# Hybrid trunk with sixteen experts: the last expert's round in an order of its own, one transfer for the state space's table, the values' weights split by channel blocks

## The chip, the core and the metric

The kernel runs on one core of a Trainium2 chip. The metric is the device time of one execution in microseconds; lower is better. The engines meant below are PE (matrix products), DVE (vector), ACT (scalar functions and copies), POOL (GpSimd, here small operations and indirect transfers) and SP (which only issues transfers). Each works through its own instructions in order and waits on semaphores for the others.

## What is computed

One layer of a decoder trunk on 1040 tokens (16 learned ones ahead of 1024) of width 1024, in float32:

```python
h = concat([meta, x])
z = rms_norm(h, norm_mix_g)
proj = z @ w_in            # conv a, conv gate, q, k, v, forget logits, state-space input
y_conv = conformer_conv(cv_a, cv_g, ...)
y_att  = forgetting_attention(q, k, v, f_lg + fgate_b)     # 8 heads of 64, causal
y_ssm  = s5_mixer(s_u, ...)                                # 16 groups of 16 channels, 64 states
h = h + concat([y_conv, rms_norm(y_att), rms_norm(y_ssm)]) @ w_out
h = h + hier_moe(rms_norm(h))    # 4 groups of 4 experts; top group, top 2 in it
return rms_norm(h, final_norm_g)[:, 16:]
# an expert: (silu(t @ w1[e]) * (t @ w3[e])) @ w2[e], weighted by its gate; FF = 256
```

## The kernel before

Every float32 product is made of three products of rounded numbers: each operand is split into a high part and the rest, and `mm3` (lines 281 to 283, one for each of the three) adds high by rest, rest by high and high by high into one bank. So every weight that comes in is first copied by ACT with rounding (the high part) and then subtracted by DVE (the rest).

**Front part.** A scheduler orders the instructions of projection, convolution, state space and attention by the priorities of the code. `load_w` loads a block of the input projection's weights and splits it: ACT line 356, DVE line 357. For the values it is called twice for each of two halves of 260 columns, each time with four blocks of 128 channels, so that one split works on 128x1040; the 24 products of each block of tokens (`KT_`, nine of them) use the channel blocks k = 0 to 7 in turn, as lines 281, 282 and 283 for each k. Between these products the scheduler puts the steps of the state space: products L1923, DVE lines 1930 to 1946, POOL lines 1932 to 1947, then products L1955 and L1958. DVE also works at the convolution there (L480).

`TT` is a table of the state space's kernel. Its 240x256 numbers are written to a scratch tensor `k_d` (L1894, L1895) and read back as eight windows that overlap, shifted by 16 rows each: eight transfers of 128 KB (L1900), each into one slice of `tj`. ACT L1901 copies the whole to `TT`, and PE's L1955 uses it.

**Experts.** The sixteen experts are worked through in an order written out by hand (`tc.manual_schedule()`), one round each. For expert e, a block b of up to 128 tokens and a half hf of the columns, the names of the steps are: f0, f1 the first products of block 0 and 1 (24 of 512 columns each); g0, g1 the gate (ACT L1289, DVE L1291 and L1292); u0, u1 the turn of the gated numbers (PE L1298); v0, v1 their split (ACT L1303, DVE L1304); w0, w1 the split of the two halves of w2 (ACT L1350, DVE L1351); s00, s01 the second products of block 0 of the expert before (6 of 512 columns each), s1 those of its block 1; e00 to e11 the evictions of the expert before (DVE L1513 in the last rounds). Block 1 is under a condition; of the last four experts (numbers 12 to 15) only expert 15 has a second block in this data.

The rows of tokens that belong to none of the last four experts go out as dense rows. The rows of experts 12 to 15 are held in tiles `hr[e]`, to which the evictions add; then each is normed (`norm_steps`: ACT L1404 squares, POOL L273 and L275 the root, DVE L1409 the product) and written with an indirect transfer of POOL (`result`, L1447). Norm steps of the rows that are ready are kept in a list `later`, and `tick(n)` takes n of them at the places that `TICKS` names. What no round takes is done behind the last round (`tick(99)`), then come expert 15's second products, its evictions, and the norms and results of experts 14 and 15.

## Time and profile before

| what | us |
|---|---|
| runs shown: median (lowest to highest of 3) | 863.53 (860.25 to 863.63) |
| the profiled execution's own time | 861.33 |
| its span in the profile | 859.7 |
| PE busy | 785.4 (91% of the span) |
| DVE busy | 592.2 (69%) |
| ACT busy | 433.5 (50%) |
| POOL busy | 243.1 (28%) |

The span is the stretch from the first to the last instruction that the profile has; the execution's own time is 1.6 us longer. Times within the trace are counted from the span's start. PE's mean granted clock is 0.964 of its full 2.4 GHz.

### The profile page before, as it was taken

Reading aid. Unit: us, or ns where it says so; the run is one execution under the profiler, and the core shown is the slowest. Engines: PE = TensorE matmul, PEld = TensorE weight load, DVE = VectorE, ACT = ScalarE, POOL = GpSimd, SP = SyncE. Lnnn points to the kernel's source line nnn. Section 1 sums busy time; section 2 is a strip of 40 time slices with the busy share of each in tenths; the row PEclk is TensorE's granted clock in tenths of the full one; section 3 lists DMA queues with packets and bytes.
Section 4 is the critical chain, followed back from the end, with each engine's and each line's share of the span. In section 5 each row is a group of like instructions: output and inputs, shape, how many; then the busy total and the mean of one; then the engine's idle time right before and its main releaser. Section 6 shows DMA issues by size and latency. Waiting matters only on the chain. (4 is left out here: it accounts for less than half of the span.)

```text
span 859.7 us, 13252 instructions
## 1 busy us (share of the span) xinstructions
PE 785.4 (91%) x4496; PEld 638.1 (74%) x4497; DVE 592.2 (69%) x1298; ACT 433.5 (50%) x788; POOL 243.1 (28%) x359
## 2 busy tenths in 40 slices
PE   6799988999999999999999999968999999897873
PEld 4698978989899955566657888846887886675652
DVE  4972898887745376666625336587779777897995
ACT  5512354434334166556564322145569565786861
POOL 2189978730001000000002110013224223223144
PEclk9999998999999999999999999978999999999985
DMA  9126131122320042012233334417699979979862
GB/s 279 33 63 125 51 99 39 30 64 73 101 74 1 13 148 99 30 70 75 74 99 80 122 123 147 148 51 256 213 296 286 279 237 267 302 242 269 323 265 108
DMA packets 88861, 121.49 MB, mean 141 GB/s; under 512 B 14828, under 2 KB 69899, under 8 KB 88786
## 3 DMA queue, kind: packets, MB, share of 16 engines
q1 hardware_dynamic: 81730, 101.46, 37.3%
q0 software_dynamic: 7056, 19.09, 8.3%
q8 instruction: 40, 0.66, 0.3%
q14 instruction: 35, 0.29, 0.1%
HBM read 100.64 MB, written 26.52 MB: 148 GB/s over the span
## 5 line engine op out<-in xcount | busy, mean ns | idle before, releaser
L281 PE MATMUL psum<-arena,arena 128*128 128x512 f32 (+6 forms) x872 | 309.4, 355 | 7.9 <-DVE arena L1513 2.4
L282 PE MATMUL psum<-arena,arena 128*128 128x512 f32 (+6 forms) x872 | 303.0, 348 | 3.4 <-DVE arena L357 3.3
L283 PE MATMUL psum<-arena,arena 128*128 128x512 f32 (+6 forms) x872 | 302.1, 348 | 0.0
L281 PEld LDWEIGHTS psum<-arena,arena 128*128 128x128 f32 (+1 forms) x872 | 166.7, 191 | 27.4 <-issue 3.9
L282 PEld LDWEIGHTS psum<-arena,arena 128*128 128x128 f32 (+1 forms) x872 | 166.9, 191 | 18.7 <-DVE arena L357 3.9
L283 PEld LDWEIGHTS psum<-arena,arena 128*128 128x128 f32 (+1 forms) x872 | 166.1, 191 | 17.2 <-DVE arena L1279 0.4
L1351 DVE TENSOR_TENSOR arena<-arena,arena 128x1024 fp32r<-128x1024 f32 x96 | 113.5, 1220 | 12.7 <-ACT arena L1350 11.9
L1350 ACT ACTIVATE arena<-arena 128x1024 fp32r<-128x1024 f32 x96 | 98.7, 1072 | 0.0
L722 DVE CUSTOM_DVE_ANT_0 arena<-psum,arena 128x144 bf16<-128x144 f32 (+6 forms) x112 | 55.2, 507 | 47.4 <-PE psum L720 24.2
L777 ACT ACTIVATE arena<-psum,arena 128x512 f32<-128x512 f32 (+4 forms) x112 | 59.2, 539 | 47.8 <-PE psum L774 30.9
L780 PE MATMUL psum<-arena 128*65 128x512 f32 (+4 forms) x224 | 82.8, 455 | 0.5 <-ACT arena L777 0.5
L273 POOL TENSOR_SCALAR arena<-arena 128x1 f32<-128x1 f32 (+2 forms) x37 | 7.9, 213 | 253.9 <-ACT arena L897 71.9
L1315 POOL DMA_INDIRECT h_d<-arena x17 | 34.1, 2007 | 126.5 <-DVE arena L1279 55.1
L1278 ACT ACTIVATE arena<-psum 128x512 fp32r<-128x512 f32 x64 | 38.4, 604 | 27.3 <-PE psum L1272 27.3
L480 DVE SCALAR_TENSOR_TENSOR psum<-arena,psum 128x1024 f32<-128x1024 f32 x40 | 51.4, 1286 | 0.7
L1279 DVE TENSOR_TENSOR arena<-psum,arena 128x512 fp32r<-128x512 f32 x64 | 43.6, 684 | 11.6 <-ACT arena L1278 11.6
L717 PE MATMUL psum<-arena 128*128 128x144 f32 (+6 forms) x112 | 51.4, 483 | 0.0
L490 POOL TENSOR_TENSOR arena<-arena 128x512 f32<-128x512 f32 x36 | 48.5, 1370 | 6.6 <-ACT arena L487 6.6
L769 PE MATMUL psum<-arena 128*128 128x512 f32 (+4 forms) x112 | 47.8, 427 | 2.7 <-ACT arena L777 2.4
L1272 PE MATMUL psum<-arena 128*128 128x128 f32 x256 | 37.8, 281 | 11.6 <-DVE arena L1279 5.2
L1272 PEld LDWEIGHTS psum<-arena 128*128 128x128 f32 x256 | 30.4, 144 | 22.6 <-DVE arena L1304 7.3
L487 ACT ACTIVATE arena<-arena 128x512 f32<-128x512 f32 x40 | 28.4, 722 | 34.6 <-POOL arena L490 24.1
(302 smaller groups left out, 1249.0 us busy)
## 6 DMA issues: line engine op xcount, KB each, us to landing
arena<-in_exp_w_dram SPq DMA_DIRECT2D x64, 512.0 KB
arena<-in_exp_w_dram SPq DMA_DIRECT2D x16, 1024.0 KB
arena<-in_x_dram SPq DMA_DIRECT2D x16, 512.0 KB
arena<-in_w_in_dram SPq DMA_DIRECT2D x14, 512.0 KB
arena<-cr_d SPq DMA_DIRECT2D x8, 520.0 KB
arena<-in_w_out_dram SPq DMA_DIRECT2D x8, 512.0 KB
h_d<-arena SPq DMA_DIRECT2D x8, 512.0 KB
t_d<-arena SPq DMA_DIRECT2D x8, 512.0 KB
```

What stands on the lines that cost most here:

```text
L281: PE.matmul(out=acc, lhsT=lh[k], rhs=rh[k], start=(k == 0), stop=False)
L282: PE.matmul(out=acc, lhsT=lh[k], rhs=rl[k], start=False, stop=False)
L283: PE.matmul(out=acc, lhsT=ll[k], rhs=rh[k], start=False, stop=(k == n - 1))
L480: V.scalar_tensor_tensor(out=yc, in0=ub[:, m, w:w + NX], scalar=cwt[:, m, w:w + 1], in1=yc, op0=OP.mult, op1=OP.add)
L490: G.tensor_tensor(out=yp[:, a:a + 512], in0=yp[:, a:a + 512], in1=o, op=OP.add)
L717: PE.matmul(out=sp, lhsT=QS[:, i * 128 - 128:i * 128], rhs=KS[:, a:b], start=True, stop=not last)
L722: V.tensor_tensor_reduce(out=jk_b()[:, :b - a], in0=sp, in1=nrow[:, a:b], scale=1.0, scalar=-3.0e38, op0=OP.add, op1=OP.max, accum_out=mp[ ...
L777: S.activation(out=pt, in_=sp, func=AF.Exp, bias=ccol[:nk, j, h:h + 1])
L780: PE.matmul(out=po[:, q0 - 512 * g:512], lhsT=vt[:nk, j, h, :], rhs=pt, start=j == 0, stop=j == last, skip_group_check=True)
L1272: PE.transpose(tp[:, k, :], xg[:, c:c + 128], ident)
L1350: S.activation(out=h[:, cs], in_=raw[:, cs], func=AF.Copy)
L1351: eng.tensor_tensor(out=l[:, cs], in0=raw[:, cs], in1=h[:, cs].bitcast(F32), op=OP.subtract)
```

## The change

Four things change.

- **The table.** The eight transfers to `tj` become one of 128x8x256, with a negative stride over the windows.
- **The values' weights.** `load_w` can split in parts. For the values it does so in four, one for each block of 128 channels (128x260), and the calls have a higher priority for the scheduler (`at_priority(-150)`).
- **The last round.** For expert 15, `ORDER` is replaced by `LAST`, in which the numbers are ticks. f1 stands behind s00, s01 and u0, and g1 stands behind w1 and s1. `late67`, which puts the norms of rows 4 to 7 and of experts 12 and 13 on the list, is called at the round's start.
- **The end.** The second products of expert 15's block 0 stand ahead of u1, the squares of 12, 13 and 14 ahead of v1, and what is left of the norms and all results of experts 12 and 13 behind the last eviction.

```diff
-    def load_w(col, n, k0=0, k1=KD, later=False):
+    def load_w(col, n, k0=0, k1=KD, later=False, parts=1):
...
         def split():
-            S.activation(out=h, in_=raw, func=AF.Copy)
-            V.tensor_tensor(out=l, in0=raw, in1=h.bitcast(F32), op=OP.subtract)
+            for i in range(parts):
+                ks = slice(kk // parts * i, kk // parts * (i + 1))
+                S.activation(out=h[:, ks], in_=raw[:, ks], func=AF.Copy)
+                V.tensor_tensor(out=l[:, ks], in0=raw[:, ks], in1=h[:, ks].bitcast(F32), op=OP.subtract)
...
     for half in (1, 0):
-        wv = [load_w(1536 + 260 * half, 260, 4 * q, 4 * q + 4) for q in range(2)]
+
+        with at_priority(-150):
+            wv = [load_w(1536 + 260 * half, 260, 4 * q, 4 * q + 4, parts=4) for q in range(2)]
...
 TICKS = (
     dict(f1=1, s00=1, g0=1, x01=1, w0=1, v0=1, e01=1, x10=2, w1=1, b0=1, b1=1, x11=1),
-    dict(f1=1, x00=1, s00=1, g0=1, t10=2, x01=1, g1=1, s01=1, v0=1, e00=1, e01=1, s1=1, x10=1,
-         t11=2, w1=1, u1=1, b0=1, b1=1, end=4),
 )
+
+LAST = "f0 2 s00 1 w0 g0 1 s01 e00 2 u0 v0 e01 1 f1 w1 2 s1 1 g1 2 e10 e11 2".split()
...
-        3: {"ga": late67},
...
-            for w in ORDER + ["end"]:
+            for w in ORDER + ["end"] if e + 1 < NE else []:
...
-        tick(99)
         e = NE - 1
+        late67()
+        for w in LAST:
+            if w.isdigit():
+                tick(int(w))
+            else:
+                steps[w][0](e)
...
+        do_second(e, 0, 0)
         do(n14[:4])
-        do_second(e, 0, 0)
         do_second(e, 0, 1)
+        do_turn_gate(e, 1)
+        tick(2)
+        do_gate_turned(e, 1)
+        do_evict(e, 0, 0)
         do_second(e, 1, None)
-        do_evict(e, 0, 0)
         do_evict(e, 0, 1)
+        tick(2)
         do(n15[0][:3])
-        do(n14[4:])
         do_evict(e, 1, 0)
         do_evict(e, 1, 1)
+        tick(99)
+        do(n15[1][:3])
+        do(n14[4:])
         for b in range(2):
             result(e - 1, b)
-        do(n15[1][:3])
         for b in range(2):
             do(n15[b][3:])
             result(e, b)
...
-        for j in range(8):
-
-            SY.dma_start(out=tj[:, j, :], in_=dram(k_d, (7 - j) * 16 * 256, [[256, 128], [1, 256]]))
+
+        SY.dma_start(out=tj, in_=dram(k_d, 7 * 16 * 256, [[256, 128], [-16 * 256, 8], [1, 256]]))
```

How the instructions stand now is shown at three places. Line numbers of the changed kernel are 2 to 12 higher: the split's DVE line 357 is 359 there, L480 is 482, L1931 to L1946 are L1943 to L1958, L1289 is L1293, L1303 is L1307, L1350 is L1354, L1404 is L1408 and L1447 is L1451.

On DVE in the front part, around the second split of the values' first half, the order before was as follows (the split is the row with 128x1040):

```order
L1943 TENSOR_TENSOR arena_61<-arena_61 128x390
L480 SCALAR_TENSOR_TENSOR psum<-arena_61,psum 128x1024
L1946 TENSOR_TENSOR arena_61<-arena_61 128x390
L480 SCALAR_TENSOR_TENSOR psum<-arena_61,psum 128x1024 x2
L1931 TENSOR_TENSOR arena_61<-psum,arena_61 128x390
L357 TENSOR_TENSOR arena_84<-arena_61,arena_83 128x1040
L480 SCALAR_TENSOR_TENSOR psum<-arena_61,psum 128x1024
```

In the changed kernel the same stretch reads:

```order
L1958 TENSOR_TENSOR arena_61<-arena_61 128x390
L359 TENSOR_TENSOR arena_84<-arena_61,arena_83 128x260
L482 SCALAR_TENSOR_TENSOR psum<-arena_61,psum 128x1024
L359 TENSOR_TENSOR arena_84<-arena_61,arena_83 128x260 x3
L1943 TENSOR_TENSOR arena_61<-psum,arena_61 128x390
L482 SCALAR_TENSOR_TENSOR psum<-arena_61,psum 128x1024 x2
```

The split has four parts, and they stand ahead of two operations (one of the convolution, L480, and L1931) that were ahead of it.

On ACT in the last round, from the gate of block 0 (the first 128x256 row, L1289) to the split of block 1's turned gate (the second L1303), the order before was as follows; rows with 128x1024 of L1350 are w0 and w1, those of L1404 are squares:

```order
L1289 ACTIVATE arena_61<-psum 128x256
L1404 ACTIVATE arena_61<-arena_61 128x1024
L1289 ACTIVATE arena_61<-psum 128x256
L1350 ACTIVATE arena_60<-arena_61 128x1024
L1303 ACTIVATE arena_2690<-psum 128x256
L1404 ACTIVATE arena_61<-arena_2879 128x1024 x2
L1404 ACTIVATE arena_61<-arena_61 128x1024 x2
L1350 ACTIVATE arena_60<-arena_61 128x1024
...
L1303 ACTIVATE arena_2690<-psum 128x256
```

In the changed kernel, from the same gate on:

```order
L1293 ACTIVATE arena_61<-psum 128x256
L1408 ACTIVATE arena_61<-arena_61 128x1024
L1307 ACTIVATE arena_2707<-psum 128x256
L1354 ACTIVATE arena_60<-arena_61 128x1024
...
L1293 ACTIVATE arena_61<-psum 128x256
L1408 ACTIVATE arena_61<-arena_2896 128x1024
...
L1408 ACTIVATE arena_61<-arena_2896 128x1024
L1408 ACTIVATE arena_61<-arena_61 128x1024 x3
...
L1408 ACTIVATE arena_61<-arena_61 128x1024
L1307 ACTIVATE arena_2707<-psum 128x256
```

Between the gate of block 1 and the split of its turned numbers stand six squares (two each of experts 12, 13 and 14); before, four squares and w1 stood there, and none of expert 14.

On POOL at the end, results of experts 12 and 13 (the first L1447 reads `arena_2879`, a tile of expert 12) stood ahead of the root for expert 14 (128x2) and for the two blocks of expert 15 (128x1):

```order
L275 TENSOR_TENSOR arena_61<-arena_61 128x4
...
L1447 DMA out_dram<-arena_2879,arena_61 1024x1024
...
L1447 DMA out_dram<-arena_61 1024x1024
...
L273 TENSOR_SCALAR arena_61<-arena_61 128x2
L275 TENSOR_TENSOR arena_61<-arena_61 128x2
...
L273 TENSOR_SCALAR arena_61<-arena_61 128x1
```

In the changed kernel the roots come first, that of expert 14 ahead of that of 12 and 13 (128x4):

```order
L275 TENSOR_TENSOR arena_61<-arena_61 128x2
L273 TENSOR_SCALAR arena_61<-arena_61 128x4
L275 TENSOR_TENSOR arena_61<-arena_61 128x4
...
L275 TENSOR_TENSOR arena_61<-arena_61 128x1
...
L1451 DMA out_dram<-arena_2896,arena_61 1024x1024
...
L1451 DMA out_dram<-arena_61 1024x1024
```

All results, those of 12 and 13 too, now stand behind the root of expert 15's first block; the root of its second block follows the results of 13.

## Rows read from the trace of the kernel before

**Rows 1.** Busy time by stretch: length, PE, PEld, DVE, ACT, POOL, PE's clock, DMA, GB/s.
```profile
300.00:400.00 100.00, 96.41 (x530) 59.03 (x529) 67.01 (x197) 62.04 (x106) 0.00 (x0) 1.00 0.23 80
```

**Rows 2.** Timeline of SP: start, duration, instruction; the table's transfers.
```profile
118.46 3.94 SPq L1900 DMA_DIRECT2D arena<-k_d  x8
```

**Rows 3.** Timeline of ACT: the table's copy, with the idle time before it.
```profile
125.40 1.91 ACT L1901 ACTIVATE arena<-arena 128x2048 f32<-128x2048 f32 x1 [2.83 <-DMA arena<-k_d]
```

**Rows 4.** Timeline of PE: the first product with the table.
```profile
127.36 0.49 PE L1955 MATMUL psum<-arena,arena 128*128 128x128 f32 x2 [3.58 <-ACT arena L1901]
```

**Rows 5.** Busy time by stretch, behind the waits of rows 4 and 9.
```profile
129.00:131.00 2.00, 2.00 (x8) 2.00 (x8) 1.10 (x1) 2.00 (x4) 0.17 (x1) 0.50 0.03 2
149.00:152.00 3.00, 3.00 (x15) 2.77 (x14) 2.96 (x4) 1.73 (x5) 2.12 (x3) 0.50 0.63 176
```

**Rows 6.** Timeline of SP: one transfer of 512 KB (128x1024) from a scratch tensor.
```profile
196.10 0.34 SPq L1984 DMA_DIRECT2D arena<-y_d  x1
```

**Rows 7.** Timeline of ACT: the operation that waits for that transfer.
```profile
199.93 1.07 ACT L1985 ACTIVATE arena<-arena 128x1024 f32<-128x1024 f32 x1 [1.96 <-DMA arena<-y_d]
```

**Rows 8.** Timeline of DVE ahead of the second split of the values.
```profile
143.63 2.60 DVE L480 SCALAR_TENSOR_TENSOR psum<-arena,psum 128x1024 f32<-128x1024 f32 x2
...
146.61 1.30 DVE L357 TENSOR_TENSOR arena<-arena,arena 128x1040 fp32r<-128x1040 f32 x1
```

**Rows 9.** Timeline of PE: the values' products before and behind the wait.
```profile
145.43 0.28 PE L281 MATMUL psum<-arena,arena 128*128 128x260 f32 x1
147.97 0.39 PE L282 MATMUL psum<-arena,arena 128*128 128x260 f32 x1 [2.25 <-DVE arena L357]
```

**Rows 10.** Timeline of DVE: the state space's next steps.
```profile
159.61 0.56 DVE L1930 TENSOR_TENSOR arena<-psum,arena 128x390 f32<-128x390 f32 x1 [3.54 <-PE psum L1923]
...
184.61 0.43 DVE L1930 TENSOR_TENSOR arena<-psum,arena 128x260 f32<-128x260 f32 x1 [0.79 <-PE psum L1923]
```

**Rows 11.** Timeline of POOL: the last step ahead of PE's L1958.
```profile
173.43 1.03 POOL L1944 TENSOR_TENSOR arena<-arena 128x390 f32<-128x390 f32 x1
```

**Rows 12.** Timeline of PE: that product.
```profile
175.63 0.71 PE L1958 MATMUL psum<-arena 64*128 64x128 f32 x4
```

**Rows 13.** Timeline of PE in the last round: first and last of f1, u1, and two second products.
```profile
820.87 0.39 PE L281 MATMUL psum<-arena,arena 128*128 128x512 f32 x1
...
826.17 0.39 PE L283 MATMUL psum<-arena,arena 128*128 128x512 f32 x1
...
831.81 0.69 PE L1298 MATMUL psum<-arena 128*128 128x128 f32 x2 [2.24 <-DVE arena L1304]
...
842.43 0.63 PE L281 MATMUL psum<-arena,arena 128*128 128x512 f32 x1
842.86 0.63 PE L282 MATMUL psum<-arena,arena 128*128 128x512 f32 x1
```

**Rows 14.** Timeline of ACT in the last round: two squares.
```profile
817.59 1.06 ACT L1404 ACTIVATE arena<-arena 128x1024 bf16<-128x1024 f32 x1
...
818.77 1.06 ACT L1404 ACTIVATE arena<-arena 128x1024 bf16<-128x1024 f32 x1
```

**Rows 15.** Timeline of DVE in the last round.
```profile
824.68 0.42 DVE L1292 TENSOR_TENSOR arena<-arena,psum 128x256 f32<-128x256 f32 x1
...
829.00 1.22 DVE L1351 TENSOR_TENSOR arena<-arena,arena 128x1024 fp32r<-128x1024 f32 x1
...
835.31 2.48 DVE L1409 SCALAR_TENSOR_TENSOR arena<-arena,arena 128x1024 f32<-128x1024 f32 x2
...
846.25 1.41 DVE L1513 SCALAR_TENSOR_TENSOR arena<-psum,arena 128x512 f32<-128x512 f32 x2
```

**Rows 16.** Timeline of POOL at the end: results of the last experts.
```profile
837.05 1.67 POOL L1447 DMA_INDIRECT out_dram<-arena,arena  x1 [2.51 <-DVE arena L1409]
...
847.66 2.13 POOL L1447 DMA_INDIRECT out_dram<-arena  x1 [0.91 <-DVE arena L1513]
...
853.25 0.96 POOL L1447 DMA_INDIRECT out_dram<-arena  x1 [0.30 <-POOLq L1618]
```

## What the change will do, forecast before it ran

> **What bounds the kernel now.** I read the page first, for where each engine is busy, then the busy times by stretch, then the timelines around the three places that the diff touches. From the values' products to the experts PE is nearly without gaps: in a typical stretch of the middle it is busy 96.41 of 100 us at full clock, and no other engine is above 68 [rows 1]. There a microsecond that PE no longer waits in the front part should come out at the end. In the last 45 us it is another matter: PE waits for DVE and ACT, and the end is set by the chain from the last eviction over the last results of POOL. The reader is to see three things: two holes in PE's work in the front part, each with a stretch of low clock behind it; the order in which ACT takes the squares in the last round; and what POOL still has to send when the last eviction is done.
>
> **The table.** The eight transfers are issued from 118.46 on, over 3.94 us [rows 2]. ACT starts its copy at 125.40, after 2.83 us of waiting for them, and takes 1.91 [rows 3]; PE then starts at 127.36, after 3.58 us of idleness [rows 4]. So from the first issue to the last landing it is 6.94 us. One issue takes 0.34 us [rows 6], so 3.6 us of issuing fall away, but the bytes stay. No row shows one transfer of 1 MB. From below: one of 512 KB took 199.93 − 196.10 = 3.83 us from its issue to the operation that waited for it [rows 6, 7]; 1 MB in that time would be here by 122.3, which gains 3.1 us at most. From above: 6.94 again, no gain. In between, half the bytes more at half that transfer's whole rate (another 1.9 us) gives 5.7, so ACT starts at about 124.2. I take 1.2 us of gain. PE still idles over 2 us then, so I leave the low clock behind it as it is (8 products in 2 us at 0.50 [rows 5]).
>
> The Trainium skill, "DMA: Bandwidth & Descriptors", section "Anatomy of one DMA — SWDGE (gpsimd) path", fits a transfer's time with a fixed 2.0 us and the bytes at 436 GB/s; for 1 MB that is 4.4 us, an estimate, and what that section measured is another queue than SP's. By that fit the gain would be 2.5 us and the total 1.3 us lower than mine. The 512 KB transfer would by that fit take 3.2 us; the trace has 3.83 [rows 6, 7], so the fit is too short here.
>
> **The values' weights.** PE waits 2.25 us at 147.97 for DVE's split of the second four channel blocks [rows 9]. That split of 128x1040 starts at 146.61 because the convolution's operations and one step of the state space stand ahead of it [rows 8]. In the new order the first part stands before the convolution's operation that started at 143.63 and the other three behind it. One operation of 260 columns takes 0.43 us at most [rows 10], so the parts are done at about 144.1 and from 145.6 to 146.4; PE, which was at 145.43 [rows 9] at the first product that needs another block, takes three products for each. So the 2.25 us go. The clock fell to 0.50 behind this wait: 15 products in 3 us [rows 5], work that at full clock is done in 1.5 us, so 1.5 us go too. The second half has smaller waits of the same kind; I take 0.4. In all 4.1 us.
>
> Against it: twelve more operations for DVE and twelve for ACT. Four of 0.43 are 1.7 us where 1.30 stood [rows 8, 10], 0.4 more for each of four splits and 1.6 over both halves. In the first half the 3.54 us in which DVE waits for PE at 159.61 hide that [rows 10]; if PE comes earlier, this cover shrinks to nothing, and DVE's convolution and state-space steps are what is late next. The second point is POOL: its last step ahead of PE's L1958 ends at 173.43 + 1.03 = 174.46, and PE came to L1958 at 175.63, only 1.2 us later [rows 11, 12]. PE that is 4 us early waits for it up to 2.8 us, unless POOL's chain, which begins behind PE's and DVE's work at 159.61, moves forward as well. I give back 0.8 us for both, with bounds of 0 and 3. **Front part: −1.2 − 4.1 + 0.8 = −4.5 us**, between −1.1 and −7.2.
>
> **The last round.** f1 began at 820.87, with f0 done, and ran without a gap: its 24 products from 820.87 to 826.17 are 0.23 apart [rows 13]. Now s00 and s01 come first (12 products, 2.8 us, to 823.6), then u0, which needs g0 from DVE. g0 was done there at 824.68 + 0.42 = 825.1, and w0's 1.22, which stood behind it at 829.00, is now ahead of it [rows 15]: u0 starts at about 826.3. PE idles 2.7 us, and f1 with the 24 products ends at 832.1. Behind an idleness of 2.24 us PE's clock was low until after 842.86, where products stood 0.43 apart [rows 13]; a spell of ten such products adds 2.0, and f1 ends at 834.1. Before, it was done at 826.6.
>
> g1 follows, then on ACT the six squares at 818.77 − 817.59 = 1.18 each [rows 14], 7.1 us in all, ahead of v1. So v1 starts at 839.7, or 841.7 with the spell. PE has only the 12 products of block 0 and u1 meanwhile, idles several microseconds, and takes the last 12 products of block 1 at 0.43 rather than 0.23 (5.2 us instead of 2.8). With DVE's two last evictions, 1.41 [rows 15], the last one is done at 848.4. At full clock the products of 12's rows on DVE set it, since 12's root is now behind 14's on POOL: squares done at 839.7, two roots of about 1 us each, two products 2.48 [rows 15], two evictions, 845.8. Before it was 846.25 + 1.41 = 847.7. **So −1.9 to +0.7; I hold the low clock to be three times as likely, +0.1.**
>
> **The end.** Before, from 847.7 to the end of the last result at 853.25 + 0.96 = 854.2 it was 6.5 us, in which POOL sent three results; those of 12 and 13 had gone ahead, the first at 837.05 [rows 16]. Now there are five results, with a root between. DVE has six products left behind the last eviction, 1.2 each [rows 15], so the last result is sent no earlier than 7.2 us behind it and takes 0.96 more: 8.2, +1.7. At the long durations (2.2 for the first, 1.8, root 0.9, then 2.2, 2.3 and 1.0, of rows that range from 0.96 to 2.13 [rows 16]) it is 10.4, +3.9. I take +2.8. **Last round and end: +2.9 us**, between −0.2 and +4.6. What lies behind the last result (5.5 us) stays.
>
> **Sum.** −4.5 + 2.9 = −1.6 us; 861.33 becomes 859.7. The profiled execution stands 2.2 us under the median of the runs shown, which I keep: 863.5 − 1.6 = 861.9.
>
> **The rivals.**
> - **The end costs nothing.** The low clock doesn't come and the results go at a microsecond each, so that DVE's products set them: −0.2 at the end, −4.5 to −6 in front, 857.5 to 859. For it: one result took 0.96 [rows 16], and PE's holes in the front part are plain. Against it: PE idles longer in the last round than where the clock fell.
> - **The squares ahead of v1 decide.** ACT's 7.1 us of squares between g1 and v1 leave PE idle and at low clock, and five results stand in series behind it: +4.6. This becomes slower than before once the front part keeps less than 4.6, as when POOL's chain takes back 2.8 and the table gives nothing (−1.3): +3.3, 866.8. For it: all prices are rows; against it: it needs POOL's chain not to move at all.
> - **The table's transfer lands no earlier**, since the bytes set it and not the eight issues: the rest as forecast, −0.4, 863.1. For it: all eight went out within 3.94 us and the last landed only 3 us later [rows 2, 3].
>
> **Chances.** My forecast (860 to 863) 0.42, the end for nothing 0.32, the squares 0.14, the table for nothing 0.12. A measurement of this kernel can tell about 0.5%, 4.3 us, from no change. Faster by more than that: 0.28 of the first rival and 0.04 of the forecast's own lower edge, 0.32. Slower by more: two thirds of the second rival, 0.10. The rest, 0.58, is within 0.5%. The range from 857 to 866 holds all but the outer parts of the two rivals.
>
> **What would show it.** One L1900 row in place of eight, ACT's copy at about 124.2, PE's idleness ahead of L1955 down from 3.6 to 2.4. No wait of PE for the values' split around 145.5 and full clock from 146 to 150. The attention's first products some 4 us earlier; if L1958 shows a wait for POOL, that part of the gain is lost there. In the last round an idle PE of some 2.7 us ahead of u0, six squares in a row, v1 about 13 us behind f1's start, and five results in a row behind the last eviction, over 8 to 10 us. I'd be wrong if DVE, relieved elsewhere, comes to g0 in time for u0, or if the scheduler's new order delays the state space by more than PE gains.

## The result

The changed kernel takes 868.62 us (median of 6 runs, 867.38 to 869.06), the kernel before 863.11 on the same chip (860.25 to 864.29): ratio 1.0067 [1.0049, 1.0084], 5.5 us slower. The forecast was 861.9, and 868.6 lies outside its range of 857 to 866. The profiled execution has a span of 866.8 us where before had 859.7, 7.1 more.

Busy times by stretch, changed kernel (stretch, length, PE, PEld, DVE, ACT, POOL, PE's granted clock, DMA share, GB/s):

```profile
72.00:80.00 8.00, 8.00 (x34) 7.88 (x33) 0.00 (x0) 0.70 (x2) 8.00 (x24) 0.50 1.22 158
100.00:150.00 50.00, 45.38 (x309) 43.62 (x307) 49.54 (x51) 26.32 (x43) 42.24 (x43) 0.97 0.22 64
129.00:131.00 2.00, 2.00 (x13) 2.00 (x12) 2.00 (x5) 2.00 (x6) 0.28 (x1) 1.00 0.03 2
149.00:152.00 3.00, 2.21 (x9) 1.61 (x9) 3.00 (x4) 0.00 (x0) 2.04 (x2) 0.50 0.00 0
320.00:335.00 15.00, 13.17 (x71) 8.40 (x69) 10.82 (x26) 10.33 (x18) 0.00 (x0) 0.89 0.46 158
830.00:850.00 20.00, 12.67 (x52) 9.11 (x52) 15.45 (x21) 9.93 (x18) 3.98 (x6) 1.00 0.40 161
```

The low clock behind the table is gone, that behind the values is not [rows 5]. It is also low at 72 to 80 us and a little at 320 to 335 (before had 1.00 from 300 to 400 [rows 1]); in the last round it stays at full speed.

Timeline of the changed kernel's front part, a selection of rows of several engines (start, duration, engine, line, operation; in brackets the idle time ahead and what ended it):

```profile
119.29 0.38 SPq L1912 DMA_DIRECT2D arena<-k_d  x1
125.00 1.91 ACT L1913 ACTIVATE arena<-arena 128x2048 f32<-128x2048 f32 x1 [1.93 <-DMA arena<-k_d]
127.59 0.49 PE L1967 MATMUL psum<-arena,arena 128*128 128x128 f32 x2
...
143.26 2.80 POOL L492 TENSOR_TENSOR arena<-arena 128x512 f32<-128x512 f32 x2
144.87 1.49 DVE L359 TENSOR_TENSOR arena<-arena,arena 128x260 fp32r<-128x260 f32 x1
146.03 1.20 POOL L1959 TENSOR_TENSOR arena<-arena 128x390 f32<-128x390 f32 x1
146.28 1.28 DVE L482 SCALAR_TENSOR_TENSOR psum<-arena,psum 128x1024 f32<-128x1024 f32 x1
146.41 0.39 PE L282 MATMUL psum<-arena,arena 128*128 128x260 f32 x1 [4.22 <-DVE arena L359]
147.20 1.01 POOL L1956 TENSOR_TENSOR arena<-arena 128x390 f32<-128x390 f32 x1
147.47 3.86 DVE L359 TENSOR_TENSOR arena<-arena,arena 128x260 fp32r<-128x260 f32 x3
148.17 2.87 POOL L492 TENSOR_TENSOR arena<-arena 128x512 f32<-128x512 f32 x2
149.97 0.59 PE L282 MATMUL psum<-arena,arena 128*128 128x260 f32 x1 [0.40 <-DVE arena L359]
151.38 0.58 PE L282 MATMUL psum<-arena,arena 128*128 128x260 f32 x1 [0.40 <-DVE arena L359]
...
222.37 0.28 PE L283 MATMUL psum<-arena,arena 128*16 128x260 f32 x1
...
588.52 1.03 PE L1276 MATMUL psum<-arena 128*128 128x128 f32 x8
```

Three things to see. The one transfer lands 5.7 us after its issue, and PE no longer waits at the table. PE's wait for the second split of the values, 2.25 us before [rows 9], is 4.22 and two of 0.40 more. And the split, 1.30 us in one piece [rows 8], is 1.49 + 3.86 = 5.35 in four, ending at 151.33 and not 147.91.

Timeline of the changed kernel's last round and end, again a selection:

```profile
819.15 0.50 PE L281 MATMUL psum<-arena,arena 128*128 128x512 f32 x1 [0.59 <-ACT arena L1282]
829.74 0.42 DVE L1296 TENSOR_TENSOR arena<-arena,psum 128x256 f32<-128x256 f32 x1
830.21 0.44 PE L1302 MATMUL psum<-arena 128*128 128x128 f32 x2 [2.46 <-DVE arena L1296]
...
836.68 1.05 ACT L1408 ACTIVATE arena<-arena 128x1024 bf16<-128x1024 f32 x1
842.59 1.06 ACT L1408 ACTIVATE arena<-arena 128x1024 bf16<-128x1024 f32 x1
843.64 0.36 ACT L1307 ACTIVATE arena<-psum 128x256 fp32r<-128x256 f32 x1
844.05 0.50 PE L281 MATMUL psum<-arena,arena 128*128 128x512 f32 x1 [2.58 <-ACT arena L1307]
848.58 1.40 DVE L1517 SCALAR_TENSOR_TENSOR arena<-psum,arena 128x512 f32<-128x512 f32 x2
849.90 6.06 DVE L1413 SCALAR_TENSOR_TENSOR arena<-arena 128x1024 f32<-128x1024 f32 x5
850.05 2.06 POOL L1451 DMA_INDIRECT out_dram<-arena,arena  x1 [0.98 <-DVE arena L1517]
852.42 1.99 POOL L1451 DMA_INDIRECT out_dram<-arena  x1 [0.31 <-DVE arena L1413]
856.42 1.28 DVE L1413 SCALAR_TENSOR_TENSOR arena<-arena 128x1024 f32<-128x1024 f32 x1 [0.47 <-POOL arena L275]
856.58 2.04 POOL L1451 DMA_INDIRECT out_dram<-arena  x1 [0.20 <-issue]
858.93 0.96 POOL L1451 DMA_INDIRECT out_dram<-arena  x1 [0.31 <-issue]
860.20 0.97 POOL L1451 DMA_INDIRECT out_dram<-arena  x1 [0.30 <-issue]
```

PE idles 2.46 us ahead of u0, ACT's six squares stand ahead of v1, and five results follow the last eviction: 11.2 us from 849.98 to 861.17, 6.5 before. A result takes 2 us while DVE's products L1413 run and 0.96 when DVE has nothing to do.

**Where the 7.1 us come from**, by the same instruction in both traces: +2.01 up to the last product of the values (220.36 before, 222.37); +1.90 from there to the experts' first turn (584.61, 588.52); +0.04 to expert 15's first product (815.20, 819.15); +3.15 from that to the end (44.50, 47.65). The row of before:

```profile
220.36 0.28 PE L283 MATMUL psum<-arena,arena 128*16 128x260 f32 x1
```

The stretch behind the front part should have been unchanged. It took 364.25 us before and 366.15 here. In the other traces of this record it takes 363.7 to 364.4 us where the clock is 1.00 from 320 to 335 (365.65 in end_alone alone), 366.4 in the changed kernel's second trace (0.89) and 368.2 in two others (0.77, experiment 7). So these 1.90 us most likely belong to the low clock there, and not to the front part; end_alone shows that something else can add as much.

### The profile page after: what moved, and what is told of

Its sections match the earlier page's. It is cut to its first block, busy times and chain, and to the rows that moved or that the text cites. A ratio compares the mean times of both kernels' runs of the same rounds, so it can differ in the third digit from the quotient of the medians.

```text
span 866.8 us, 13267 instructions
## 1 busy us (share of the span) xinstructions
PE 790.7 (91%) x4496; PEld 641.6 (74%) x4497; DVE 601.4 (69%) x1310; ACT 434.5 (50%) x800; POOL 241.8 (28%) x359
## 5 line engine op out<-in xcount | busy, mean ns | idle before, releaser
L1354 ACT ACTIVATE arena<-arena 128x1024 fp32r<-128x1024 f32 x96 | 98.7, 1072 | 0.0
L482 DVE SCALAR_TENSOR_TENSOR psum<-arena,psum 128x1024 f32<-128x1024 f32 x40 | 51.2, 1281 | 0.7
L359 DVE TENSOR_TENSOR arena<-arena,arena 128x260 fp32r<-128x260 f32 (+1 forms) x30 | 36.7, 1245 | 11.2 <-ACT arena L358 11.1
```

The lines of the kernel that those rows point to most:

```text
L482: V.scalar_tensor_tensor(out=yc, in0=ub[:, m, w:w + NX], scalar=cwt[:, m, w:w + 1], in1=yc, op0=OP.mult, op1=OP.add)
L1354: S.activation(out=h[:, cs], in_=raw[:, cs], func=AF.Copy)
```

## The experiments

Theory after the result: the end costs what was forecast, and the front part loses because each of the small splits waits for an operation of POOL. Rivals: the table's transfer or the scheduler's new order loses the time, or it is the number of operations alone. Each run was compared with the kernel before on its own chip; "wait" is PE's at the second split of the values' first half.

**1. One part of the change at a time.** The kernel before with only the single transfer (table_alone, and the same once more as table_twice); with only `load_w`'s parts and priority (values_alone); with only `LAST` and the end (end_alone).

> The kernel before with the one transfer for the table and nothing else. Theory (the forecast's): PE's wait at the table's first product falls from 3.6 to about 2.2 us, since the copy on ACT starts some 5.7 us behind the issue and not 6.9; the time falls by about 1 us, which this comparison can hardly tell. Rival (bytes set the landing): the copy starts no earlier than 6.9 us behind the first issue and nothing changes.

> The kernel before with the values' weights split in four parts at the higher priority, and nothing else. Theory (DVE's parts wait for POOL, one by one): each part of 128x260 that meets a POOL operation takes 1.0 to 1.5 us in place of 0.42, so the three parts behind the convolution's operation last about 3.8 us; PE waits 4 to 5 us at the second four channel blocks in place of 2.25, with low clock behind it; the time rises by 2 to 3 us. Rival (the forecast's: a part costs 0.43 and the wait goes): the time falls by 3 to 4 us. A second rival, that the 3 us more which the changed kernel loses at low clock around 70 to 82 us come from the higher priority of these loads: then this run shows the low clock there too, and the one with the new end alone doesn't.

> The kernel before with the new order of the last round and the end, and nothing else. Theory: it costs what the end of the changed kernel showed, some 3 us: 2.5 us of PE waiting for g0 behind w0, six squares ahead of v1, five results behind the last eviction over 10 to 11 us in place of three over 6.5. Rival (the loss lies in the front part alone): no change within 1 us.

> The kernel with the table's single transfer alone, run again. Theory (the scheduler's new order on DVE in the second half puts scans and a product of the state space ahead of the splits, so PE waits some 2.4 us there where it waited 1.0): 1 to 3 us above the kernel before again, with that wait in the profile. Rival (the first comparison was chance): no difference, and the wait is gone.

| run | us | before | ratio |
|---|---|---|---|
| table_alone | 866.64 | 864.0 | 1.0036 [1.0009, 1.0064] |
| table_twice | 867.56 | 864.16 | 1.0041 [1.0024, 1.0059] |
| values_alone | 867.37 | 864.0 | 1.0050 [1.0028, 1.0073] |
| end_alone | 867.03 | 864.0 | 1.0034 [1.0008, 1.0060] |

Each part alone makes the kernel slower. That the table does was a surprise, and it repeated. Two waits of PE show how. At the values PE, which no longer waits at the table (table_alone) or waits 2.13 us there (table_twice), waits 4.65 and 4.04 us where it waited 2.25. The kernel before itself waits some 4.6 us at the values in executions in which it doesn't wait at the table (experiment 6), so only traces with the same arrival can be compared: PE, held up by POOL for 3.93 and 3.66 us at 70 us, at a clock of 0.79 from 72 to 80 in both, waits 3.14 at the table and 2.33 at the values with the eight transfers (end_squares_early, whose front part is that of before), 2.13 and 4.04 with one (table_twice). And in the values' second half a new wait has come; DVE and PE in table_twice:

```profile
189.50 0.43 DVE L1942 TENSOR_TENSOR arena<-arena 128x260 f32<-128x260 f32 x1
189.85 1.27 DVE L1937 TENSOR_TENSOR_SCAN arena<-arena 128x130 f32<-128x130 f32 x2
191.04 1.21 DVE L357 TENSOR_TENSOR arena<-arena,arena 128x1040 fp32r<-128x1040 f32 x1
192.31 0.39 PE L282 MATMUL psum<-arena,arena 128*128 128x260 f32 x1 [2.40 <-DVE arena L357]
```

The scheduler now has steps of the state space ahead of the split, and PE waits 2.40 us (2.42 in table_alone) where two waits of about 0.5 were. So a transfer that lands earlier moves PE's wait to DVE's splits. That DVE sets the pace there is an inference from these waits: DVE's busy time from 100 to 150 us (44.16 of 50 before, 49.54 in the changed kernel) doesn't show it, since it is 43.4 to 48.5 over the traces with the front part of before, 44.10 in table_twice and 45.43 in the changed kernel's second trace.

**2. Does a split wait for POOL?** The changed kernel without POOL's sums of the convolution, one execution. It leaves out those sums, so that other tokens go to other experts; only its front part is compared.

```diff
-                    if w > 31 - NPT:
-                        G.tensor_tensor(out=yp[:, a:a + 512], in0=yp[:, a:a + 512], in1=o, op=OP.add)
```

> The changed kernel without POOL's sums of the convolution, which leaves part of the convolution out; one look, for the durations. Theory (a DVE operation of two operands in SBUF waits for a POOL operation that is under way, once for each instruction): the parts of 128x260 take 0.42 us wherever no POOL operation overlaps them, and the second split's three parts some 1.1 us together in place of 3.86; PE's wait of 4.2 us there goes or falls under 1 us. Rival (parts are slow for their own sake, or for ACT or the transfers beside them): they stay at 1.0 to 1.5 us each.

Its time was 865.07. DVE around the same split:

```profile
139.53 0.42 DVE L359 TENSOR_TENSOR arena<-arena,arena 128x260 fp32r<-128x260 f32 x1
139.87 1.28 DVE L482 SCALAR_TENSOR_TENSOR psum<-arena,psum 128x1024 f32<-128x1024 f32 x1
141.07 1.10 DVE L359 TENSOR_TENSOR arena<-arena,arena 128x260 fp32r<-128x260 f32 x3
```

POOL has no operation there, and the four parts take 0.42 and 1.10 in place of 1.49 and 3.86. PE doesn't wait for them, and the experts begin at 578.62, not 588.52 (the run also lacks the rest of what those sums cost, so these 10 us are not the splits' alone). The theory's part on POOL holds, and the changed kernel's own trace bears it out: its parts at 128.75 and 130.03, with no POOL operation under way, take 0.42 us, and the four of the second split 1.49, 1.03, 1.50 and 1.49 while POOL is without a gap from 143.26 to 151.04. In the values' second half, where POOL's operations are shorter, parts beside POOL take 0.86 to 0.97 and one 0.40. L482, which reads PSUM and SBUF, takes 1.28 us in both kernels.

The Trainium skill, "SBUF — State Buffer", section "Who interferes with whom", says that a DVE instruction with two inputs in SBUF contends with a GpSimd instruction that reads SBUF, through a port pair that one of them locks for its whole instruction. The trace agrees: 0.42 against 1.03 to 1.50.

**3. How many parts?** Four and two parts at the old priority in the kernel before (parts_alone, two_parts), and one and two parts in the changed kernel.

```diff
-        wv = [load_w(1536 + 260 * half, 260, 4 * q, 4 * q + 4) for q in range(2)]
+        wv = [load_w(1536 + 260 * half, 260, 4 * q, 4 * q + 4, parts=4) for q in range(2)]
```

In the others `parts=4` is 2 or 1.

> The kernel before with the values' weights split in four parts, at the old priority. Theory (each part that meets a POOL operation waits for it, and the first parts let PE go on earlier): the parts cost DVE 2 to 4 us more than one split did, PE gets back a part of that, and the time is 0 to 3 us above the kernel before. Rival (the higher priority, not the parts, is what cost time): the time is at or under the kernel before's.

> The kernel before with the values' weights split in two parts (128x520) at the old priority. Theory (every part waits for a POOL operation under way, so the cost goes by the number of parts): each of the second split's two parts takes 1.2 to 1.5 us where 0.7 would do without POOL, the last one is done some 1 to 1.5 us later than the single split was and 1.5 to 2 us earlier than with four parts, relative to the product of the state space's step ahead of it; the time is 0 to 2 us above the kernel before. Rival (the amount of data sets the time, not the number of parts): both parts together take 1.3 to 1.5 us.

> The changed kernel with the values' weights split in one part (128x1040) as before, but still at the higher priority. Theory (it is the number of parts that costs, since every part waits for POOL anew): the second split takes about 1.3 us, PE's wait of 4.2 us at the second four channel blocks falls to 2 or less, and the time is 2 to 3 us below the changed kernel's, 865.5 to 866.5. Rival (it is the priority, which puts the splits in a worse place): the wait stays at 4 us or so and the time at 868 to 869.

> The changed kernel with two parts of 128x520 in place of four, all else as in the change. Theory (the number of parts costs, since each waits for POOL): the second split's two parts take 2 to 2.8 us together in place of 5.3, PE's waits there (4.2 and twice 0.4) fall to 2 or less, and the time is 2 to 4 us under the changed kernel's: 1 to 3.5 us above the kernel before. Rival (the higher priority or the order around it): no more than 1 us under the changed kernel's, 5 us above the kernel before.

| run | us | before | ratio | split: DVE busy, end | wait |
|---|---|---|---|---|---|
| parts_alone | 867.23 | 865.34 | 1.0037 [1.0018, 1.0056] | 5.26, 151.25 | 3.60 |
| two_parts | 863.21 | 864.16 | 0.9986 [0.9962, 1.0011] | 2.01, 148.95 | none over 0.4 |
| after_one_part | 870.98 | 864.0 | 1.0097 [1.0067, 1.0128] | 1.52, 149.39 | 4.66 |
| after_two_parts | 869.64 | 864.74 | 1.0062 [1.0040, 1.0084] | 2.97, 150.56 | 3.67 |

In the kernel before this fits: four parts lose, two don't. DVE's two pieces there, of which only the second ran long. The first began at the same time as POOL's L1949 (145.83), and there POOL's operation was the long one, 1.58 us where L1946 behind it took 1.02:

```profile
145.83 0.69 DVE L359 TENSOR_TENSOR arena<-arena,arena 128x520 fp32r<-128x520 f32 x1
147.63 1.32 DVE L359 TENSOR_TENSOR arena<-arena,arena 128x520 fp32r<-128x520 f32 x1
```

But in the changed kernel neither one nor two parts are faster than four (1.0067). That the number of parts alone makes the changed kernel's loss fell here: with one part PE waits 4.66 us at the first half and 2.58 at the second, as with the table alone.

**4. The whole front part** with the end of before:

> The kernel before with both front edits, the single transfer and the four parts at the higher priority, and the old order of the last round and the end. Theory (the end costs 3 us of the 5.5): 2 to 3.5 us above the kernel before, with PE waiting about 4.2 us at the second split and twice 0.4 for its last parts, and f0 of the last expert to the span's end 44.5 us as before. Rival (the two parts of the change act on each other, so that the front part costs nothing by itself): no difference.

864.94 against 864.16, ratio 1.0006 [0.9993, 1.0019]. Expected were 2 to 3.5 us. Table and values together cost 0.5 us (0.06%), alone they cost 3.1 to 3.5 and 4.3 (0.36%, 0.41%, 0.50%): the parts don't add. The waits at the first half don't explain it, since front_both has as long a split as the changed kernel (5.34, to 153.46) and waits of 3.97, 0.46, 0.40 and 0.40. With end_alone (0.34%) it makes 0.40%, less than the 0.67% of the changed kernel, which has both. The low clock at 320 us may be what is missing: both traces of the changed kernel have it (some 1.9 us), those of front_both and end_alone don't; whether the timed runs had it is not known.

**5. The end.** The kernel before with only the results of 12 and 13 behind the last eviction (results_last); the new last round with the squares of 12 and 13 ahead of g1 and v1 ahead of 14's (end_squares_early); the same with the results of 12 sent ahead of 14's root and those of 13 ahead of the last evictions (end_results_early). The core of each edit:

```diff
-                later.append(lambda k=k, i=i: result(late + k, i))
+                held.append(lambda k=k, i=i: result(late + k, i))
...
         do_evict(e, 1, 1)
+        do(held)
```

```diff
-LAST = "f0 2 s00 1 w0 g0 1 s01 e00 2 u0 v0 e01 1 f1 w1 2 s1 1 g1 2 e10 e11 2".split()
+LAST = "f0 2 s00 1 g0 w0 1 s01 e00 2 u0 v0 e01 1 f1 w1 2 s1 6 g1 e10 e11 3".split()
```

```diff
         do_gate_turned(e, 1)
+        for b in range(2):
+            result(late, b)
         do(n14[:4])
...
         tick(99)
+        for b in range(2):
+            result(late + 1, b)
         do_evict(e, 1, 0)
```

> The kernel before, with only the results of experts 12 and 13 moved behind the last eviction. Theory (results stand in series on POOL): two more results of 1 to 2 us each behind the last eviction and ahead of that of expert 14, so the span's end moves by 2 to 4 us. Rival (they are hidden behind DVE's last products): no change within 1 us.

> The kernel before with the last round in yet another order: as in the change, but g0 ahead of w0, the four squares of 12 and 13 ahead of g1 (while ACT waits for f1), v1 ahead of the squares of 14, products and results of 12 and 13 ahead of the last eviction. Theory (what cost time in the change's end is w0 ahead of g0, squares ahead of v1 and the late results): PE's wait for u0 falls from 2.5 to about 1.2 us, the last eviction is done near 844 and three results follow it: 2 to 4 us below the kernel before, 5 to 6 below the one with the change's end alone. Rival (DVE's amount of work, the same in any order, sets the end): within 1 us of the kernel with the change's end alone.

> As the last order tried for the end (squares early), with the result of 12 ahead of the root of 14 on POOL and that of 13 ahead of the last eviction. Theory (POOL's queue held the two results back until 847 though 12's rows were ready at 840.3): only three results stand behind the last eviction, the root for 15's second block is done some 3 us earlier, and the last result ends 3 to 4 us earlier than in that order: 1.5 to 4 us below the kernel before. Rival (DVE's last products set it): no more than 1 us below that order, at or above the kernel before.

Times from expert 15's first product, in the profile: to the end of the last eviction, from there to the end of the last result, and to the end of the span.

| run | last eviction | last result | span's end | us | before | ratio |
|---|---|---|---|---|---|---|
| before | 32.46 | 6.55 | 44.50 | | | |
| the changed kernel | 30.83 | 11.19 | 47.65 | 868.62 | 863.11 | 1.0067 [1.0049, 1.0084] |
| end_alone | 32.75 | 9.43 | 48.33 | 867.03 | 864.0 | 1.0034 [1.0008, 1.0060] |
| results_last | 32.41 | 10.05 | 47.90 | 868.32 | 864.37 | 1.0043 [1.0028, 1.0058] |
| end_squares_early | 28.90 | 11.17 | 45.81 | 865.58 | 864.37 | 1.0015 [0.9999, 1.0031] |
| end_results_early | 27.98 | 10.24 | 43.99 | 864.56 | 865.34 | 0.9999 [0.9975, 1.0024] |

Held results alone cost 3.4 us of the span and 3.7 timed (0.43%): most of the end's loss is theirs. In end_squares_early the last eviction is 3.6 us earlier than before; how much of this the squares give isn't shown, since the same order has g0 ahead of w0 (PE waits 0.90 us for u0, not 2.46). In end_results_early the result of 12 goes ahead of the last eviction, that of 13 begins 0.5 us behind it, and the end no longer costs anything. Both orders were expected to be faster than before, by 2 to 4 and 1.5 to 4 us; neither is. POOL in results_last, where the pattern of 2 us and 0.96 recurs:

```profile
847.99 2.08 POOL L1447 DMA_INDIRECT out_dram<-arena,arena  x1 [0.98 <-DVE arena L1513]
850.37 0.98 POOL L1447 DMA_INDIRECT out_dram<-arena  x1 [0.30 <-issue]
852.33 0.96 POOL L1447 DMA_INDIRECT out_dram<-arena  x1 [0.98 <-DMA arena<-h_d,arena]
...
854.70 2.00 POOL L1447 DMA_INDIRECT out_dram<-arena  x1 [0.24 <-issue]
857.00 0.96 POOL L1447 DMA_INDIRECT out_dram<-arena  x1 [0.30 <-POOLq L1619]
```

**6. The same kernels again**, one execution each: the kernel before twice, the changed kernel once.

> The kernel before, unchanged, profiled again. In its first profile and in that of the kernel with the new end alone, PE's clock was low for some 3 to 4 us behind the wait at 70 us; in the four profiles of kernels with a changed front part it was low for 8 to 10 us, which costs 3 us more, though the kernel with the table's transfer alone issues the same instructions on every engine up to 118 us. Theory: the length of this spell is chance, so this profile may show either, and the same kernel's PE then comes to the table 3 to 4 us later and waits little or nothing there. Rival: the spell belongs to the changed front part, and is 3 to 4 us long here again.

> The kernel before, unchanged, profiled a third time, for the spread of its front part. Theory (the length of the spell of low clock behind 70 us is chance, and what PE loses or saves there comes back at the waits for the table and the values): whatever the spell, PE's last product with the table lies between 195 and 198 us and the experts' first turn between 584 and 588. Rival: the front part's end follows the spell one to one, 3 to 4 us apart.

> The changed kernel, unchanged, profiled again, for the same. Theory (DVE's work, stretched by POOL, sets the pace from 90 to 150 us): PE waits again 4 us or more for the second split of the values, and if the spell behind 70 us is short, PE waits for the table's transfer again, about 3 us. Rival (the transfer alone takes the table's wait away): no wait at the table with a short spell.

Their times were 865.67, 870.35 and 871.1. From expert 15's first product to the end it is 44.46, 44.46 and 47.19: the end's cost is the same each time. The front is not. The kernel before waited 0 and 0.25 us at the table, since PE came late: it waited 3.61 and 3.93 us for POOL at 70 us, where it had waited 1.96 in its first trace, and its clock was low for longer behind that wait. The stretch from 72 to 80 us in the first profile of before and in before_again:

```profile
72.00:80.00 8.00, 8.00 (x49) 8.00 (x48) 0.49 (x1) 0.60 (x1) 8.00 (x23) 0.88 1.18 161
```

```profile
72.00:80.00 8.00, 7.26 (x32) 7.16 (x33) 0.71 (x1) 1.20 (x2) 8.00 (x21) 0.50 1.22 160
```

When PE comes late there, it waits 4.61 at the values in place of 2.25 (before_again):

```profile
149.94 0.39 PE L282 MATMUL psum<-arena,arena 128*128 128x260 f32 x1 [4.61 <-DVE arena L357]
```

The changed kernel has the long spell in its first profile (0.50) and a shorter one in after_again (0.79), where PE waits 1.58 at the table. What the table's transfer gives at its place therefore depends on when PE comes: 1.0 us in the like pair of experiment 1 (3.14 to 2.13), nothing where PE comes late. Whether the spell is chance stays open. In the twelve traces in which PE waits 1.93 to 2.05 us at 70 us, the clock from 72 to 80 is 0.85 to 1.00 in the six with the front part of before or with two parts at the old priority, and 0.50 or 0.51 in the six others; that sorts by kernel, although the work and the order of all engines are the same up to 118 us in before, table_alone and the changed kernel. before_third went against what was expected of it: PE's last product with the table was only at 204.43 and the experts began at 593.5, in part since one more wait of 3.46 us for DVE had come at 116.82.

The traces of all experiments, put together, give the front part's length without the wait at 70 us: from that wait's end to the last product of the values.

| front part | traces | us |
|---|---|---|
| as before | 6 | 149.7 to 151.9 |
| as before, with the wait at 116.82 (before_third) | 1 | 156.3 |
| as changed (after, after_again, front_both) | 3 | 150.9 to 152.7 |
| the single transfer alone | 2 | 153.2, 154.2 |
| four parts (values_alone, parts_alone) | 2 | 154.0, 153.9 |
| two parts, old priority (two_parts and experiment 7) | 3 | 146.5 to 147.2 |

This agrees with the times: each edit alone costs about 3 us, both together about 1, and two parts gain some 4.

**7. The better parts together**: two parts at the old priority and the end of end_results_early, twice.

> The kernel before with two parts at the old priority and the best order tried for the end (results early). Theory (the two don't touch each other): 1 to 2.5 us below the kernel before, from up to 2 us in front and 0.5 at the end. Rival (what is won in front is lost in the waits of the last round): no difference.

> Two parts at the old priority and the best order tried for the end, compared once more. Theory (front and end each give a little): 1 to 3 us below the kernel before again. Rival (the first comparison was chance): no difference, or slower.

862.32 against 864.74, 0.9978 [0.9950, 1.0005], and 860.83 against 863.45, 0.9985 [0.9954, 1.0016]. Both medians are some 2.5 us below before, and both intervals just include 1. The two profiles of this one kernel differ by 5.7 us (862.6 and 856.9), and 4.2 of it arises in the attention (last product of the values to the experts: 368.2 and 364.0). From 320 to 335 us, first the one and then the other:

```profile
320.00:335.00 15.00, 13.85 (x58) 8.46 (x59) 8.49 (x24) 8.45 (x15) 0.00 (x0) 0.77 0.32 105
```

```profile
320.00:335.00 15.00, 14.06 (x73) 8.28 (x71) 9.86 (x31) 9.59 (x17) 0.00 (x0) 1.00 0.35 115
```

The granted clock there was 0.77 and 1.00, behind PE's waits for ACT of 0.47, 0.48 and 0.94 us in the first and 0.19, 0.47 and 0.94 in the second. Over all traces the spell came in four (both of the changed kernel are among them) of the nine where the first of these waits was over 0.4 us, and in none where it was shorter. Why that wait differs from one execution to the next is open. One such spell takes back nearly as much as the front's edits were to give (4.5). Two of the three traces with two parts have it, which may be how a front part that is some 4 us shorter in all three comes out at only 0.14% in two_parts.

## Why the prediction was wrong

**The step that failed** is "One operation of 260 columns takes 0.43 us at most [rows 10], so the parts are done at about 144.1 and from 145.6 to 146.4". That row has one operand in PSUM. The parts, with both operands in SBUF, took 1.03 to 1.50 us each beside POOL and 0.42 without it (experiment 2), and were done at 146.36 and 151.33. The trace of before had shown it: DVE's L1943 and L1946, both 128x390 from SBUF, took 0.53 and 1.44 us, the second beside a sum of POOL that began just ahead of it (DVE's two rows, then POOL's):

```profile
140.62 0.53 DVE L1943 TENSOR_TENSOR arena<-arena 128x390 f32<-128x390 f32 x1
142.27 1.44 DVE L1946 TENSOR_TENSOR arena<-arena 128x390 f32<-128x390 f32 x1
...
142.01 2.85 POOL L490 TENSOR_TENSOR arena<-arena 128x512 f32<-128x512 f32 x2
```

So the 4.1 us at the values were not gained: PE waits 4.22 + 0.40 + 0.40 where 2.25 was (4.6 in traces of before without a wait at the table), and the low clock stayed. With two parts at the old priority the wait all but goes (0.53 us at most), and the front part is some 4 us shorter (experiments 3 and 6).

**The step behind it**, that "a microsecond that PE no longer waits in the front part should come out at the end", failed as well. What PE gains at the table it waits at the next split (1.0 us less at the table, 1.7 more at the values in the like pair of experiment 1) and at that of the second half (2.40 us); and what is left is within what the clock's spells at 72 and 320 us add or take. I had read [rows 1], a stretch behind the front part in which DVE is busy 67 of 100 us, for a front part in which it is busy 44.16 of 50.

**The table's landing** was right: 5.7 us forecast and measured. Its gain was not (1.0 us or nothing at its place; the kernel slower by 0.4%). The fit of the Trainium skill ("DMA: Bandwidth & Descriptors", section "Anatomy of one DMA — SWDGE (gpsimd) path") gave 4.4 us for this transfer; the trace has 5.7, so it was too short again.

**Front part in all:** forecast −4.5, bounds −7.2 to −1.1; measured +0.5 (front_both, timed), and +2.0 at the last product of the values in the two profiles, where traces of one and the same front part differ as much. Shown are the parts' waits and the wait that moves from table to values; why table and values together cost less than either alone is open.

**Last round and end:** forecast +2.9, measured +3.15 in the profile and +2.9 timed alone (0.34%). That the sum fits is luck: its two terms were each off, and cancelled. The last eviction came 1.6 us earlier (forecast +0.1, bounds −1.9 to +0.7): PE idled 2.46 us ahead of u0, about as forecast (2.7), but no low clock followed. It did behind 2.24 us before [rows 13], where two more waits of 1.91 and 2.39 us (to 834.41 and 839.70), not counted in the forecast, came in the same spell, and in end_alone behind 2.47. The tail was 4.6 longer (forecast +2.8, bounds +1.7 to +3.9): the root between the results took 2.2 us with its gaps (854.41 to 856.58) where I had 0.9, and the gaps of 0.3 us between the results were not in the sum.

**The rivals.** The end was not for nothing. The squares did not decide: v1 at 843.64 cost PE 2.58 us, and the last eviction was early all the same. The table's transfer did land earlier. Slower came true through a mechanism that no rival named, the splits' wait for POOL.

**What was to show it:** one transfer, an idle PE ahead of u0, six squares in a row, v1 13.1 us behind f1's start (830.54 to 843.64) and five results over 11 us are there. No wait at 145.5 and full clock at 150 are not. L1958 didn't wait for POOL in the changed kernel; the wait that the 0.8 us of give-back stood for came in values_alone and parts_alone, with 1.38 and 1.34 us at 198.

## What to carry to other kernels

Before dividing a DVE operation with two SBUF operands into pieces, look at what POOL does at that time, and take the price from a row with the same operands beside a busy POOL: here four pieces took 5.35 us for 1.30, two took 2.0 to 3.0. Ask of every wait that goes which engine paces the stretch; if it isn't the one that waited, the wait turns up at its next product. And profile the same kernel more than once before pricing a wait: 3.58 us at the table in one trace was 0 and 0.25 in two others of the same kernel.

## What the runs showed of the hardware

- **DVE beside POOL:** 128x260 from SBUF takes 0.42 us alone and mostly 0.86 to 1.50 while POOL has operations under way (once 0.40); an operation with a PSUM operand (L482) keeps its 1.28.
- **Results sent by POOL:** 0.96 to 0.98 us with DVE idle; 0.98 to 2.13 where one or two of DVE's products with both operands in SBUF run beside them; and 4.08 beside three such products, in each of the three traces with this order of the end (end_results_early, two_parts_end, two_parts_end_again, whose row, L1449, is below). The Trainium skill, "SBUF — State Buffer", section "SBUF: two separate sides", tells of DMAs from GpSimd's queue that can't write their descriptors while DVE runs an operation of a mode that takes the shared ports. The trace agrees in direction, 0.96 against 2 and more; no row here shows in which mode DVE's products run.

```profile
841.34 4.08 POOL L1449 DMA_INDIRECT out_dram<-arena  x1 [0.29 <-issue]
```

- **The clock behind nearly the same wait** differs between traces: behind 1.96 us of idleness at 70 us it was 0.88 of full speed from 72 to 80 in before, behind 1.93 it was 0.50 in the changed kernel. In the last round it stayed at 1.00 behind 2.46 us in the changed kernel and was 0.50 from 830 to 832 behind 2.47 us in end_alone, which has the same order there.
